# A hybrid decoder layer on one Trainium2 core: later heads' loads ordered behind the last chunk's transfers, a rope table per block, and a re-planned instruction order

## The chip, the core and the metric

The kernel runs on 1 core of one Trainium2 chip. The core has five engines that run side by side: TensorE (PE in the profile, with PEld for its weight loads), VectorE (DVE), ScalarE (ACT), GpSimd (POOL) and SyncE (SP), which in this kernel issues nearly all DMA transfers. Every transfer goes through 16 shared DMA engines. The metric is the time of one execution in microseconds; lower is better.

## The reference

One layer of a decoder on 2048 tokens of width 1024, all in float32:

```python
a   = rmsnorm(x, norm_pre_mix)
proj = a @ w_in                       # 1024 -> 1960 columns
h_ml  = mlstm_chunkwise(silu(conv(qk)), v, gates)        # 4 heads, recurrent over chunks
q = rmsnorm(c_q) @ w_uq ; kv = rmsnorm(c_kv) @ w_ukv     # 8 heads, rope on 32 of 96 columns
h_mla = causal softmax attention(q, k, v)
x = x + rmsnorm(concat(h_ml, h_mla) @ w_out, norm_post_mix)
x = x + rmsnorm(relu(rmsnorm(x) @ w_up)**2 @ w_down, norm_post_mlp)
```

## The kernel before

**Number format.** A float32 product is made of three TensorE passes: each operand is split into a rounded part (`hi`, cast on ACT) and the remainder (`lo`, a subtraction on DVE or POOL), and `mm3` (L225) adds hi·hi, hi·lo and lo·hi. So each loaded weight costs an ACT cast and a DVE or POOL subtraction before TensorE can use it.

**Stages.** (1) Input projections and mLSTM, in four blocks of 512 tokens (`b` = 0 to 3). A block has 16 units of weight columns (`unit`, `values`), small products for q, k and v of the attention heads (`operands`: tiles `kp`, `vp`, `qp`, `rp`), and four recurrent chunks of 128 tokens (`chunk`, L1141). Results for the heads are staged in four `sg` buffers (tiles `ks`, `vs`, `qs`, `rs`) and stored to DRAM (`qkd`, `vd`, `qrd`). (2) Attention over 8 heads × 4 query blocks: row maxima first (`maxima`, tile `m`), then scores `S`, two exponentials on ACT, a low part on DVE or POOL, and the products with `V`. (3) Output projection. (4) The two MLP products.

**The rope table.** `rope_tables` (L1288) computes sines and cosines in two halves `q`, each of which holds two blocks; it stores them to `trigd` (L1334) and spreads them into a table `trep` for all 2048 tokens with six DMAs per half (L1341, 1 MB per half). Each block later reads its part into `tb` (L820).

**The last chunk.** Chunk (3,3) needs the rows `E` (L1157, `load_e`) and `iw` (L1165, `load_w`), broadcast from DRAM. `E` has two buffers, freed by the numerators (L1192, L1193) of two chunks before; `iw` has one, freed by `scale_q` (L1186) of the chunk before. ACT then makes the exponentials (L1172). When the last chunk has ended, `switch3` (L1409) closes its buffers and opens those of the scores `S`.

**Head loads.** `load_qk` (L1495) brings q and k of one head and block into SBUF with three DMAs, `load_v` (L1508) brings V of two key tiles of 128 tokens, for four heads at once, and `matrix` (L1828) loads rows of w_out. All are issued by SP, in one queue, in program order.

**What sets the order.** Nothing runs in the order it is written. Every step is registered with `pl.op(engine, ns, function, after, key, take, free, kb)` (L137): an engine, an assumed duration, what it must follow, a due time (`key`), and the buffers it takes and frees. `Plan.run` (L147) simulates the engines with these durations and issues, for each engine, the operation that can start first, and of several that can, the one with the lowest key. The order that comes out is pinned for PE, ACT, DVE and POOL (`pin`, L236); each engine then works through its list strictly in that order, and so does the DMA queue of SP. The assumed durations thus decide the order but not the real times. Due times of stage 1 come from `kA(b, t)` (L297), which is `KEYA + (b*BLOCK + t)/1.8`.

Of the kernel before, what the change touches and what calls it, by code (L numbers as in the profile page):

```python
# [10 lines left out]
F32 = mybir.dt.float32  # L11
# [7 lines left out]
P = 128  # L19
# [3 lines left out]
TB = 512  # L23
# [10 lines left out]
HB_ = 4  # L34
LB_ = 4
# [17 lines left out]
LEAD = 20.0  # L53
VLEAD = 6.0
# [3 lines left out]
BLOCK = 123.0  # L58
XLEAD = 20.0
WLEAD = 22.0  # L60
SPLIT = 10.0
XS0 = 12.0
XS1 = -60.0
CHUNK = 2.0
# [4 lines left out]
LGAIN = 20.0  # L69
CPOOL = True  # L70
KPOOL = ()
VPOS = (2, 2, 2, 4)
KROT = 50.0
# [10 lines left out]
WSTORE = 10.0  # L84
# [38 lines left out]
class Plan:  # L123


    HOP, DMA, RATE, SUM = 190.0, 1900.0, 359.0, 4900.0
    late = 0.0

    def __init__(self):
        self.ops, self.rings, self.frees = [], {}, {}  # L130
        self.group, self.groups = None, {}
# [5 lines left out]
    def op(self, eng, ns, fn, after=(), key=0.0, take=(), free=(), kb=0):  # L137


        i = len(self.ops)  # L140
        self.ops.append((eng, ns, fn, list(after), key, take, kb))
# [5 lines left out]
    def run(self):  # L147
# [24 lines left out]
        left, moved = len(ops), 0.0  # L172
        while left:
# [31 lines left out]
            end[i] = at[eng] = s + ops[i][1]  # L205
# [12 lines left out]
def trunk(ctx: ExitStack, tc: tile.TileContext, x, xT, pos, wu, wout, wup, wdn, cols, rows, consts, edge, out, dbg=None):  # L218
# [48 lines left out]
    trep = dram.tile([P, 2, SEQ], F32, tag="trep", name="trep")  # L267
# [29 lines left out]
    def kA(b, t):  # L297

        return KEYA + (b * BLOCK + t) / 1.8
# [66 lines left out]
    def xsplit(b):  # L366
        def pair(j):
# [24 lines left out]
            for s in [slice(0, 1), slice(1, 2)] if b == 0 else [slice(0, 2)]:  # L392
                a = pl.op("SP", 500, lambda s=s: load(s), [first], key=kA(b, 0.65 * (2 * j + s.start) - 3 - XLEAD), kb=256 * (s.stop - s.start))
                for k in range(2 * j + s.start, 2 * j + s.stop):
                    at = kA(b, 0.65 * k - 3)
                    c = pl.op("Activation", 690, lambda k=k: hi(k), [a, o_col], at, take=(f"xh{k}",))
                    d = pl.op("DVE", 700, lambda k=k: lo(k), [c], at, take=(f"xl{k}",), free=[] if here else [("awr", first)])
# [44 lines left out]
    def wsplit(b, u):  # L442
# [27 lines left out]
        for s in pieces:  # L470
            n = s.stop - s.start
            a = pl.op("SP", 500, lambda s=s: load(s), [a0_], key=kA(b, at - WLEAD + WHALF * len(first)), kb=n / 2)
            c = pl.op("Activation", n * 0.833 + 110, lambda s=s: hi(s), [a], kA(b, at - SPLIT), take=() if first else ("wh",))
            d = pl.op(
                "Pool" if slow else "DVE", 148 + 2.104 * n if slow else n / 0.96 + 69, lambda s=s: lo(s), [c] + ([d] if first else []), kA(b, at - SPLIT), take=() if first else ("wl",),
# [127 lines left out]
    def latents_in(b):  # L603
# [4 lines left out]
        def one(i):  # L608
# [32 lines left out]
            if b == 0:  # L641
                o = pl.op("Activation", 560, evac, [u["op"], *t.get("o", [])], key, take=take, free=[("mm", u["head"])])
                head = o
                o = pl.op("DVE", 660, norm, [o, o_rsbc[b]], key, free=[("rsbc", o_rsbc[b])])
# [40 lines left out]
        def split(i):  # L685
# [8 lines left out]
            g = pl.op("DVE", 710, lambda: gain(i), [l, o], late, free=[("cbc", l)])  # L694
# [10 lines left out]
    def operands(b, t, o_c, held):  # L705
# [112 lines left out]
        def table():  # L818
            tb["t"] = e2.tile([P, 2, TB], F32, tag="cbc", name=f"tb{b}", bufs=1)
            dma(tb["t"], trep[:, :, bs])  # L820

        o_tb = pl.op("SP", 500, table, [o_rope[2 * (b % 2) + 1], t["gained"]], kA(b, TIME[b][18] - 10), take=("cbc",), kb=512)
# [46 lines left out]
    def rotate(b, t, G):  # L869
# [26 lines left out]
        g = pl.op("SP", 500, load, [o_rope[2 * (b % 2)], G], key, take=("cth",), kb=128)  # L896
# [149 lines left out]
    def conv(b, j):  # L1046
# [39 lines left out]
        for i in range(1, 4):  # L1086
            o = pl.op("DVE", 720, lambda i=i: tap(i), [o], key, free=[("raw", r)])
# [1618 lines left out]
```

## Time and profile before

| | us |
|---|---|
| median of 3 runs (lowest to highest) | 2447.58 (2446.93 to 2453.14) |
| profiled execution, its own time | 2449.75 |
| span of that execution in the trace | 2447.8 |
| PE busy | 2384.2 (97%) |
| DVE busy | 1766.5 (72%) |
| ACT busy | 1360.5 (56%) |
| POOL busy | 835.1 (34%) |

An engine's busy time is the time in which at least one of its instructions ran. A matmul of 128x512 lasts about 0.4 us in the profile, but the next one starts while it drains; the profile's PEclk says what share of full speed TensorE's clock was granted. In the views quoted below, a timeline row gives the start, the duration (of all instructions merged into the row), the engine, the line, the operation and, in brackets, how long the engine stood idle before it and who released it. A windows row gives busy time and instruction count of each engine in a stretch, then the granted clock, the busy share of the DMA engines and their GB/s.

### The profile page before, as it was taken

The page shows a single profiled execution, that of the slowest core. Times are in us where ns is not written, and L with a number is a line of the kernel's source. Part 1 is how long each engine was busy: PE and PEld are TensorE (multiplying, and loading weights), DVE is VectorE, ACT ScalarE, POOL GpSimd, SP SyncE. Part 2 cuts the span into 40 slices and gives each one's busy share as a digit, 9 for nine tenths or more (in the row PEclk, how much of TensorE's full clock was granted, in tenths as well). Part 3 has the DMA queues.
Part 4 walks back from the last instruction along what each step waited for, and adds up shares of the span by engine and source line. Part 5 has one row for each costly group of instructions (what it writes and reads, how often), then busy time and mean ns, then how long its engine had stood idle before and what let it go on. Part 6 is the DMA issues. An engine that isn't in the chain of part 4 may idle for free.

```text
span 2447.8 us, 34049 instructions
## 1 busy us (share of the span) xinstructions
PE 2384.2 (97%) x10915; PEld 1918.2 (78%) x10915; DVE 1766.5 (72%) x3153; ACT 1360.5 (56%) x2645; POOL 835.1 (34%) x713
## 2 busy tenths in 40 slices
PE   8899999999999999999999999999999999999998
PEld 6777787777777777788887888888888888888886
DVE  6766666648888888744866677766666687687889
ACT  5545444436777777644665666756665344343455
POOL 3433434436888788632100000000000232322346
PEclk9999999998999999999999999999999999999999
DMA  6696969797322220466777788756664534535348
GB/s 241 223 314 214 327 231 325 251 257 179 93 58 67 56 53 12 111 211 217 264 209 207 227 281 246 220 171 180 198 195 140 182 126 148 159 125 183 126 132 183
DMA packets 341819, 449.20 MB, mean 184 GB/s; under 512 B 34908, under 2 KB 227432, under 8 KB 341640
## 3 DMA queue, kind: packets, MB, share of 16 engines
q1 hardware_dynamic: 337704, 440.16, 58.2%
q0 software_dynamic: 3936, 6.87, 2.0%
q8 instruction: 86, 1.41, 0.2%
q14 instruction: 93, 0.76, 0.1%
HBM read 295.97 MB, written 153.05 MB: 183 GB/s over the span
## 4 chain that ended last, share of the span: by engine, by line
PE 78%; DVE 7%; DMA 6%; issue 3%; ACT 3%; POOL 2%; SPq 1%; DVEq 0%; ACTq 0%; POOLq 0%
PE mm L226 3%; PE mm L227 3%; PE mm L228 3%; PE S L226 3%; PE o L1622 2%; PE S L227 2%; PE S L228 2%; PE o L1625 2%; PE m L1537 2%; PE mv L227 1%; PE mv L228 1%; PE mv L226 1%; PE op L226 1%; PE op L228 1%; PE op L227 1%
## 5 line engine op out<-in xcount | busy, mean ns | idle before, releaser
L2516 POOL TENSOR_TENSOR y<-vd_0X,y 128x512 f32<-128x512 f32 x7 | 11.3, 1620 | 727.7 <-ACT vd_0X L2513 709.8
L1636 POOL TENSOR_TENSOR t<-t,ph 128x512 f32<-128x512 f32 (+1 forms) x192 | 214.4, 1116 | 17.8 <-ACT ph L1601 7.8
L1601 ACT ACTIVATE ph<-S 128x512 fp32r<-128x512 f32 (+1 forms) x320 | 170.2, 532 | 87.2 <-PE S L228 33.4
L2428 ACT CAST hh<-hr 128x512 fp32r<-128x512 f32 (+1 forms) x208 | 116.2, 567 | 150.5 <-DMA hr<-hd 23.8
L1609 DVE TENSOR_TENSOR pl<-S,ph 128x512 fp32r<-128x512 f32 (+3 forms) x272 | 156.7, 590 | 30.3 <-ACT S L1605 27.7
L226 PE MATMUL mm<-xh,wh 128*128 128x512 f32 x384 | 160.3, 417 | 17.1 <-ACT wh L458 8.4
L227 PE MATMUL mm<-xl,wh 128*128 128x512 f32 x384 | 151.7, 395 | 1.5 <-DVE xl L388 1.5
L228 PE MATMUL mm<-xh,wl 128*128 128x512 f32 x384 | 151.6, 395 | 0.7 <-DVE wl L463 0.7
L2433 DVE TENSOR_TENSOR hl<-hr,hh 128x512 fp32r<-128x512 f32 (+1 forms) x208 | 130.2, 637 | 28.2 <-ACT hh L2428 21.6
L1542 DVE TENSOR_REDUCE mp<-m 128x1 f32<-128x512 f32 x192 | 128.6, 681 | 27.1 <-PE m L1537 27.0
L1605 ACT ACTIVATE S<-S 128x512 f32<-128x512 f32 (+3 forms) x272 | 141.0, 519 | 0.3
L226 PE MATMUL S<-QK 97*128 97x512 f32 (+1 forms) x320 | 122.9, 384 | 6.2 <-DVE pl L1609 4.1
L1622 PE MATMUL o<-ph,V 128*128 128x512 f32 (+1 forms) x320 | 121.0, 378 | 0.2 <-DVE ot L1695 0.2
L1537 PE MATMUL m<-QK 96*128 96x512 f32 (+3 forms) x320 | 113.3, 399 | 6.8 <-ACT vext L1110 2.7
L227 PE MATMUL S<-QK 97*128 97x512 f32 (+1 forms) x320 | 118.3, 370 | 0.0
L228 PE MATMUL S<-QK 97*128 97x512 f32 (+1 forms) x320 | 117.9, 368 | 0.0
L1625 PE MATMUL o<-pl,V 128*65 128x512 f32 (+1 forms) x320 | 114.8, 361 | 0.2
L226 PEld LDWEIGHTS mm<-xh,wh 128*128 128x128 f32 x384 | 73.1, 190 | 38.3 <-ACT wh L458 8.4
L226 PE MATMUL op<-wo,hh 128*128 128x512 f32 x256 | 101.2, 395 | 0.7 <-DVE x L1937 0.7
L2267 ACT ACTIVATE t<-t 128x512 f32<-128x512 f32 x96 | 60.6, 631 | 73.8 <-DVE t L2262 73.2
L228 PE MATMUL op<-wo,hl 128*128 128x512 f32 x256 | 99.9, 390 | 0.0
L227 PE MATMUL op<-wo,hh 128*128 128x512 f32 x256 | 99.8, 390 | 0.0
(6442 smaller groups left out, 7581.2 us busy)
## 6 DMA issues: line engine op xcount, KB each, us to landing
hr<-hd SPq DMA_DIRECT2D x100, 448.0 KB
wr<-in_wu_dram SPq DMA_DIRECT2D x71, 512.0 KB
hd<-t SPq DMA_DIRECT2D x128, 256.0 KB
hd<-ts SPq DMA_DIRECT2D x96, 256.0 KB
wl<-wparts SPq DMA_DIRECT2D x45, 512.0 KB
QK<-qkd SPq DMA_DIRECT2D x32, 512.0 KB
xt<-in_x_dram SPq DMA_DIRECT2D x28, 512.0 KB
xf<-xd SPq DMA_DIRECT2D x40, 256.0 KB
```

The source lines that it names most:

```text
L226: pe.matmul(o, ah, bh, start=start, stop=False)
L227: pe.matmul(o, ah, bl, start=False, stop=False)
L228: pe.matmul(o, al, bh, start=False, stop=stop)
L1537: pe.matmul(ps[:, :n], Qh[s][0:96, q0 : q0 + P], Kh[s][0:96, kb * TB : kb * TB + n], start=True, stop=True)
L1542: vec.tensor_reduce(mp["t"][:, j, kb : kb + 1], ps, axis=AX.X, op=ALU.max)
L1601: act.activation(t["h"][:, :w], t["S"][:, :w], AF.Exp)
L1605: act.activation(t["p"][:, :w], t["S"][:, :w], AF.Exp)
L1609: (pool if by_pool else vec).tensor_tensor(t["l"][:, :w], t["p"][:, :w], f32(t["h"][:, :w]), ALU.subtract)
L1622: pe.matmul(o0, v[:, 0:128], t["h"][:, :w], start=start, stop=stop)
L1625: pe.matmul(o1, v[:, 64:129], t["l"][:, :w], start=start, stop=stop)
L1636: pool.tensor_tensor(to, to, hv, ALU.add)
L2433: vec.tensor_tensor(t["l", m][:, :w], t["r", m][:, :w], f32(t["h", m][:, :w]), ALU.subtract)
```

## The change

Four groups of edits:

1. **Order of loads.** `load_qk` of head 0 for blocks 1 to 3 and `load_v` of key tiles 4 to 7 are placed after the `E` and `iw` loads of chunk (3,3). V of key tiles 8 and up (heads 0 to 3) is placed after the first scores of an earlier query block of head 0, V of heads 4 to 7 after the first scores of head 2, and the first four rows of w_out after the first scores of head 4. These are orders for the planner; the data don't need them.
2. **Rope table.** `trep` becomes four tables of 512 tokens. The six spreading DMAs per half disappear from `rope_tables`; each block spreads its own part with three DMAs (512 KB) shortly before it loads it.
3. **Stage 1 due times.** The hi and lo parts of the weights of block 0 get a due time 20 units of `t` earlier (`SPLIT0`), the gains and low parts of the latents (`LGAIN`) and the rotation of the rope key (`KROT`) a later one, the rotation of block 0 moves from DVE to POOL (`KPOOL`); evacuations of stage 1 get an earlier due time (`EV`).
4. **Planner and buffers.** One more buffer for `ph` and for `pl` in the attention (`HB_`, `LB_`), other lead times, a lower assumed DMA rate, and a rule that a DVE operation marked `DVES` takes longer while POOL runs an operation of 1100 ns or more. Some 30 operations in all stages are marked so.

```diff
-HB_ = 4
-LB_ = 4
+HB_ = 5
+LB_ = 5
-LEAD = 20.0
-VLEAD = 6.0
+LEAD = 25.0
+VLEAD = 3.0
-BLOCK = 123.0
+BLOCK = 119.0
+SPLIT0 = 30.0
-CHUNK = 2.0
+CHUNK = 0.0
-LGAIN = 20.0
+LGAIN = 40.0
-KPOOL = ()
+KPOOL = (0,)
-KROT = 50.0
+KROT = 90.0
-WSTORE = 10.0
+WSTORE = 5.0
-EV = 8.0
+EV = 15.0
-PQ = 0.0
+PQ = 5.0
...
-    HOP, DMA, RATE, SUM = 190.0, 1900.0, 359.0, 4900.0
+    HOP, DMA, RATE, SUM = 190.0, 1900.0, 345.0, 4900.0
+    BESIDE, HEAVY = 0.75, 1100.0
...
+            ns = ops[i][1]
+            if i in self.shared and pool_end > s:
+                both = min(pool_end - s, ns / (1 - self.BESIDE))
+                ns += self.BESIDE * both
+            end[i] = at[eng] = s + ns
+            if eng == "Pool" and ns >= self.HEAVY:
+                pool_end = s + ns
+                if last_shared > s:
+                    at["DVE"] = max(at.get("DVE", 0.0), last_shared) + self.BESIDE * (last_shared - s)
...
-    trep = dram.tile([P, 2, SEQ], F32, tag="trep", name="trep")
+    trep = [dram.tile([P, 2, TB], F32, tag=f"trep{b}", name=f"trep{b}") for b in range(NB)]
...
+            split = SPLIT if b else SPLIT0
-            c = pl.op("Activation", ..., lambda s=s: hi(s), [a], kA(b, at - SPLIT), ...)
+            c = pl.op("Activation", ..., lambda s=s: hi(s), [a], kA(b, at - split), ...)
-                "Pool" if slow else "DVE", ..., kA(b, at - SPLIT), ...
+                "Pool" if slow else "DVES", ..., kA(b, at - split), ...
...
+        def spread():
+            for x, r0, g0, n in ((0, 0, 0, 8), (1, 48, 0, 4), (1, 32, 4, 4)):
+                to = trep[b].rearrange("(g j) x t -> g j x t", j=16)[g0 : g0 + n, :, x]
+                dma(to, trigd[r0 : r0 + 16, bs].rearrange("(o j) t -> o j t", o=1).broadcast_to((n, 16, TB)))
-        o_tb = pl.op("SP", 500, table, [o_rope[2 * (b % 2) + 1], t["gained"]], kA(b, TIME[b][18] - 10), take=("cbc",), kb=512)
+        o = pl.op("SP", 1800, spread, [o_rope[b % 2], t["gained"]], kA(b, TIME[b][18] - 25), kb=512)
+        o_tb = pl.op("SP", 500, table, [o, t["gained"]], kA(b, TIME[b][18] - 10), take=("cbc",), kb=512)
...
-        e = pl.op("SP", 500, load_e, [o_sc_in[b, "wd"]], key, take=("E",), kb=256)
-        i = pl.op("SP", 1000, load_w, [o_sc_in[b, "wd"]], key, take=("iwbc",), kb=128)
+        e = out["e"] = pl.op("SP", 500, load_e, [o_sc_in[b, "wd"]], key, take=("E",), kb=256)
+        i = out["i"] = pl.op("SP", 1000, load_w, [o_sc_in[b, "wd"]], key, take=("iwbc",), kb=128)
...
-        o = pl.op("SP", 1500, load, [..., o_s3 if s else o_s1, *war], key, kb=640)
+        o = pl.op("SP", 1500, load, [..., o_s3 if s else o_s1, *war, *(o_last if b and not h else [])], key, kb=640)
+    o_last = [o_chunk[NB - 1, 3]["e"], o_chunk[NB - 1, 3]["i"]]
...
-        o_v[g, t] = [pl.op("SP", 1000, load, [..., *([o_s3, o_const["v"]] if g else [o_s2, o_const["v0"]])], key, kb=512)]
+        if g:
+            after = [o_s3, o_const["v"], o_sc[start_of[2, qb]]]
+        else:
+            after = [o_s2, o_const["v0"], *([o_sc[start_of[0, qb - 2]]] if qb > 1 else o_last if qb else [])]
+        o_v[g, t] = [pl.op("SP", 1000, load, [o_vd[t], o_vd[t + 1], *after], key, kb=660)]
...
-        a = pl.op("SP", 500, load, [o_s3 if early else o_left], key, take=("wr",), kb=512)
+        a = pl.op("SP", 500, load, [o_sc[start_of[4, 0]] if early else o_left], key, take=("wr",), kb=512)
```

The old `spread` in `rope_tables` (L1336 to L1341, L1355) is taken out.

More of the change, by code (lines that the diff above doesn't have):

```diff
@@ L894, in lo @@
             eng.tensor_tensor(t["Gr"][s], t["G"][s], t["tg"][s], ALU.subtract)
-        g = pl.op("SP", 500, load, [o_rope[2 * (b % 2)], G], key, take=("cth",), kb=128)
+        g = pl.op("SP", 500, load, [o_rope[b % 2], G], key, take=("cth",), kb=128)
         o = pl.op(*cost, d1, [g, G], key)
@@ L1090, in conv @@
         o_qk[b, j] = [
-            pl.op("DVE", 670, lambda i=i: put(i), [h, *war, *(o_fill3 if j < 2 else [])], key, free=[("cy", y), ("cth", h)])
+            pl.op("DVES", 670, lambda i=i: put(i), [h, *war, *(o_fill3 if j < 2 else [])], key, free=[("cy", y), ("cth", h)])
             for i in range(2 if j < 2 else 1)
@@ L2106, in factor @@
         b = pl.op("Activation", 610, hi, [a, opened], key, take=(f"x{i}{kk}h",))
[L2107 removed]
+        c = pl.op("DVES", 690, lo, [b], key, take=(f"x{i}{kk}l",), free=[("xr", a)])
         o_xo[g, i, kk] = [b, c, None]
```

105 lines of the change are left out of this document (52 added, 53 removed).

## The prediction

> **What bounds the kernel.** I read the page's totals first, then busy time by stage, then the list of PE's waits, then the granted clock around the longest waits.
>
> ```profile
> PE 2384.2 (97%) x10915; PEld 1918.2 (78%) x10915; DVE 1766.5 (72%) x3153; ACT 1360.5 (56%) x2645; POOL 835.1 (34%) x713
> ```
> ```profile
> 0.00:138.00 138.00, 116.63 (x511) 92.44 (x512) 95.09 (x184) 72.33 (x133) 54.68 (x54) 0.96 0.71 242
> 138.00:520.00 382.00, 370.08 (x1709) 294.39 (x1708) 239.35 (x492) 178.24 (x346) 154.26 (x139) 1.00 0.80 275
> 520.00:580.00 60.00, 53.96 (x239) 41.70 (x238) 38.60 (x106) 22.21 (x66) 21.40 (x28) 0.83 0.96 231
> 580.00:990.00 410.00, 404.03 (x2072) 307.30 (x2071) 341.60 (x772) 318.49 (x663) 335.46 (x289) 1.00 0.27 63
> 990.00:2370.00 1380.00, 1372.29 (x6101) 1128.55 (x6101) 980.09 (x1501) 723.56 (x1318) 216.59 (x150) 1.00 0.61 187
> ```
> ```profile
> PE mv L227 <- DVE wl L463: 4.9, 2, 3.3
> PE mm L226 <- ACT vs L784: 4.3, 1, 4.3
> PE m L1537 <- ACT vext L1110: 2.7, 1, 2.7
> ```
>
> TensorE is the bound, and the change takes no matmul away. So all it can win is PE's idle time and the time at a reduced clock. Idle is 21.4 us in the first 138 us (the start among them, which stays), 11.9 us up to 520, 6.0 us up to 580, 6.0 us in the attention and 7.7 us up to 2370. These three longest waits after the start fall on places that the change touches. The clock after them:
>
> ```profile
> 64.00:71.00 7.00, 5.42 (x13) 3.69 (x13) 6.86 (x10) 1.80 (x5) 2.79 (x3) 0.52 0.89 268
> 129.00:132.00 3.00, 3.00 (x9) 2.32 (x8) 2.54 (x3) 2.66 (x5) 1.24 (x2) 0.50 0.71 157
> 538.00:542.00 4.00, 1.21 (x7) 0.73 (x5) 1.21 (x2) 3.21 (x13) 2.44 (x5) 0.97 0.96 271
> 542.00:548.50 6.50, 5.91 (x20) 5.14 (x21) 4.53 (x15) 0.00 (x0) 0.83 (x1) 0.50 1.17 294
> 548.50:555.50 7.00, 5.29 (x22) 2.71 (x20) 6.60 (x23) 2.55 (x11) 1.01 (x1) 0.99 0.78 207
> 555.50:569.00 13.50, 13.04 (x39) 9.49 (x40) 8.27 (x20) 4.44 (x11) 3.10 (x7) 0.50 0.94 221
> ```
>
> Each of these waits is followed by a stretch at half clock, which costs about half of the busy time in it: 5.42 × 0.48 = 2.6 us, 1.5 us, 5.91/2 = 3.0 us and 13.04/2 = 6.5 us. So a wait of 3 to 4 us costs more than itself.
>
> **A. Weight splits of block 0.** In the values unit TensorE stands twice for the low parts `wl`:
>
> ```profile
> 53.37 1.05 ACT L458 CAST wh<-wr 128x1024 fp32r<-128x1024 f32 x1 [1.38 <-PE mm L227]
> 55.95 1.41 DVE L681 SCALAR_TENSOR_TENSOR cca<-cca,col,cbc 128x512 f32<-128x512 f32 x2
> 57.27 3.48 DVE L1078 SCALAR_TENSOR_TENSOR qbd<-cth,cy 64x512 f32<-64x512 f32 x2
> 60.78 2.18 DVE L463 TENSOR_TENSOR wl<-wr,wh 128x1024 fp32r<-128x1024 f32 x1
> 65.49 1.22 DVE L463 TENSOR_TENSOR wl<-wr,wh 128x1024 fp32r<-128x1024 f32 x1
> 58.48 3.40 POOL L692 TENSOR_TENSOR cl<-cca,ch 128x512 fp32r<-128x512 f32 x2
> L1078 DVE SCALAR_TENSOR_TENSOR qbd<-cth,cy x16: 671/690/1790, 48.4 to 475.5; 64x512 f32<-64x512 f32 x16
> ```
>
> The cast was done at 54.4, but DVE first made gains (1.41) and two `qbd` writes (3.48). The earlier key puts `wl` ahead of both, so the first wait (3.3) goes. The second weight's cast waits for a buffer that TensorE frees, so I leave the second wait. Of the 2.6 us at half clock I take half: 3.3 + 1.3 = 4.6, say **4.5 us won**. Bounds: nothing (what DVE leaves for later delays chunk 0 as much) to 4.9 + 2.6 = 7.5. No instruction is added here.
>
> Moving the four rotation steps of block 0 to POOL frees DVE of 4 × 0.69 us (the median `qbd` row is the nearest) and gives POOL 4 × 1.3 to 1.7 us (the `cl` row: 3.40 for two). The rows also show a price: beside those `cl` steps a `qbd` write took 1.7 us instead of 0.69. If each moved step stretches one DVE step by 1.1 us, DVE loses 4.4 − 2.8 = 1.6 us. With 43 us of DVE idle in this stage and a later due time, I take 0 for it, between −2.8 and +1.6. [...]
>
> **B. Rope table.** At 112 us the second half's six DMAs stand ahead of the stores that free the `sg` buffers, and at 86 us the first half's stand ahead of an `E` load:
>
> ```profile
> 86.31 4.51 SPq L1341 DMA_DIRECT2D trep<-trigd  x6
> 112.45 4.51 SPq L1341 DMA_DIRECT2D trep<-trigd  x6
> 117.26 1.27 SPq L763 DMA_DIRECT2D qkd<-ks  x2
> 115.96 1.30 POOL L739 TENSOR_TENSOR ks<-ks 128x512 fp32r<-128x512 f32 x1
> ```
> ```profile
> 91.91 7.16 DMA E<-wd
> 117.92 9.13 DMA qkd<-ks
> ```
> ```profile
> 99.09 1.28 ACT L1172 ACTIVATE E<-E,tm 128x128 f32<-128x128 f32 x4 [2.59 <-DMA E<-wd]
> 127.17 0.69 DVE L787 COPY vs<-vp 128x512 f32<-128x512 f32 x1 [2.32 <-DMA qkd<-ks]
> ```
>
> DVE waits for the landing of a store that took 9.13 us, behind 1 MB of table. Without it SP is free at 112.5 and the store has only its own data (done at 117.3) and other transfers to wait for. The `E` landing of 7.16 us, behind another 1 MB, is the nearest row for the same queue with half the table; I put the store's landing 3 us lower. So of the 4.3 us wait 3 goes, 1.5 of clock behind it, and 0.5 at 99 us, where ACT idled 2.59 us: **5.0 us won**, bounds 0 and 4.3 + 1.5 + 0.8 = 6.6.
>
> The cost: blocks 1 to 3 get three DMAs each, 4.51/2 = 2.3 us of SP's queue and 512 KB, in a stretch whose DMA engines are 0.80 busy. The queue delays whatever store or load is next by up to 2.3 us, three times 2.3 = 6.8 at most, and 0 where a load has its usual lead. I take **1.0 us lost**.
>
> **C. The last chunk.** This is the largest term.
>
> ```profile
> 524.73 0.60 PE L1193 MATMUL num<-C,qs 128*128 128x258 f32 x2
> 525.42 1.54 POOL L1186 TENSOR_TENSOR qs<-qbd,iwbc 64x256 f32<-64x256 f32 x2 [1.12 <-PE num L1193]
> 528.37 0.60 SPq L1499 DMA_DIRECT2D QK<-qkd  x1
> 529.01 1.36 SPq L1501 DMA_DIRECT2D QK<-qrd  x2
> 531.09 0.45 SPq L1157 DMA_DIRECT2D E<-wd  x1
> 538.00 1.28 ACT L1172 ACTIVATE E<-E,tm 128x128 f32<-128x128 f32 x4 [9.44 <-DMA E<-wd]
> 540.63 0.68 ACT L1110 ACTIVATE vext<-mv,rsx 128x512 f32<-128x512 f32 x1
> 537.12 0.39 PE L228 MATMUL mv<-wh,xl 128*128 128x512 f32 x1
> 544.90 1.07 PE L1192 MATMUL num<-vext,E 128*128 128x129 f32 x4
> 558.20 0.73 PE L226 MATMUL S<-QK 97*128 97x512 f32 x1
> ```
>
> Chunk 1's numerators free the `E` buffer at 525.3. The load is issued at 531.09, behind head loads, and lands at 538.0, 6.9 us later; ACT, which works in order, stands 9.44 us, with `vext` of the last values queued behind it, and TensorE's 2.7 us wait is for that `vext`. With the new order `E` goes at 525.4 and lands by 525.4 + 6.9 = 532.3 at the latest. Then TensorE's values (until 537.5) set the pace: `vext` by 538.6, the numerators at 538.7 instead of 544.90, so 6.2 us sooner. The chain from there to the first scores (558.20 − 544.90 = 13.3 us) stays, some of it at half clock. Of the 9.5 us that the two half-clock stretches cost I take 0.3, as small, scattered products remain: **9.0 us won**. The bound is all idle from 538 to 569 (2.8 + 0.6 + 1.7 + 0.5) and all 9.5 of clock: 15.0. The other bound is 0.
>
> What is moved behind: a head load is 0.60 + 1.36 = 2.0 us of SP. Three of them now follow `iw`, which can go when POOL's scaling ends at 527.0; so they are issued from about 528.4 to 534.3 and land, at 6.9 us, by 541, when maxima and the last chunk run. Cost 0 to 3, I take **0.5 lost**. V of later heads and w_out leave a stretch with a DMA share of 0.96; their use comes more than 100 us later, under 404 us of TensorE work, at a share of 0.27, so I price them at nothing; uncovered, one load would cost its landing, 7 us.
>
> **D. The rest.** More `ph` and `pl` buffers can win at most the attention's 6.0 us of idle; I take **1.0 won**. The new planner costs reorder DVE, ACT and POOL everywhere. No row prices that: from half the idle of 138 to 520 and of the attention won (−9) to as much lost (+9). I take **1.5 lost**, since each removed delay leaves the next buffer or evacuation to be waited for. After 990 TensorE idles 7.7 us in 1380, so reordering there has little to win.
>
> Sum: −4.5 − 5.0 + 1.0 − 9.0 + 0.5 − 1.0 + 1.5 = −16.5 us. Against the profiled execution's own 2449.75 (span 2447.8 and 1.95 around it) that is 2433.2; the median of the runs lies 2.2 below that execution, so **2431 us**.
>
> **The rivals.**
> 1. *The half clock stays.* The scattered small products throttle TensorE without a long wait. Before the stretch from 555.5 the seven us hold 1.7 us of idle in all, and yet half clock followed: that speaks for it. Then A is worth 3.3, B 3.5, C 6.2, and the sum is −11.0: 2437. [...]
> 2. *All of it goes.* A, B and C near their upper bounds (6.5, 6, 13), with the costs as above: −25.5 + 2 − 3 of the attention, about 2421. The stretches at half clock follow the waits closely, which speaks for it; that chains of small steps remain at 545 to 558 speaks against it.
> 3. *The waits move.* DVE has to do the same steps before chunk 0, so A is 0; half the table still precedes the `E` load, so B is 2; the last chunk's long chain keeps C at 5. With the costs 1.0 + 0.5 + 1.5 and no gain in the attention: −4, 2443.5. DVE 6.86 busy of 7.0 at 64 to 71 speaks for it.
> 4. *The queue blocks the heads: slower.* Head 0's blocks 1 to 3 now stand in SP's queue behind `iw`. If that load goes no sooner than 534 (3 us after the present `E`), they are issued until 540.5 and land at 541 to 547.5; TensorE, done with values at 537.5, has only block 0's maxima and the chunk, stands 5 us and runs the next 13.5 us at half clock as now. With C at +7, A and B moved elsewhere (0) and 3 of costs: about +10, 2457. It decides from `E` issued at 531 or later. Against it: the buffer is free at 525.3, and the planner sees that.
>
> **How the numbers follow.** A difference below 0.3% (7.3 us: 2440.2 to 2454.9) can't be told from no change here. Forecast 0.44; rival 1 0.13, rival 2 0.11, rival 3 0.18, rival 4 0.14. Faster: 0.44 + 0.13 + 0.11 = 0.68. Same: 0.18. Slower: 0.14. The forecast's own range is 2422 to 2440; to hold 8 in 10 it must reach to rivals 1 to 3 with the ±9 of the reordering: 2413 to 2452, with rival 4 left out above and the sum of all upper bounds (2408) below.
>
> **What would show it.** A: the `wl` wait of 3.3 us gone and the clock 1.00 from 64 to 71. B: no wait for `vs` near 124, and three table DMAs per block. C: `E` of the last chunk issued within 1 us of the numerators that free it, ACT's 9.44 us gone, the first scores near 542 on a span that is then some 9.5 us shorter by A and B. It would be wrong if the first scores come at 555 or later, if new PE waits above 2 us appear in blocks 1 to 3, or if the attention's idle time grows.

## The result and the profile after

The changed kernel takes 2427.85 us (median of 6 runs, 2425.71 to 2429.46); the kernel before took 2448.38 beside it (6 runs, 2446.93 to 2453.14). The ratio is 0.9912, 95% interval 0.9900 to 0.9925: 20.5 us faster, 3.2 below the forecast of 2431 and inside its range. The profiled span fell from 2447.8 to 2426.0.

First the totals of the changed kernel's page and its windows by stage. The windows are cut where its stages lie, some 20 us earlier than before towards the end.

```profile
PE 2370.5 (98%) x10915; PEld 1915.0 (79%) x10915; DVE 1749.6 (72%) x3149; ACT 1360.6 (56%) x2645; POOL 833.4 (34%) x717
```
```profile
0.00:138.00 138.00, 123.60 (x555) 97.95 (x555) 106.71 (x191) 80.48 (x145) 64.41 (x62) 1.00 0.75 249
64.00:71.00 7.00, 7.00 (x32) 5.51 (x31) 6.88 (x11) 4.75 (x11) 1.69 (x3) 1.00 0.94 281
520.00:580.00 60.00, 56.08 (x266) 42.94 (x266) 47.33 (x125) 32.92 (x80) 30.84 (x34) 0.89 0.87 200
535.37:549.02 13.65, 13.20 (x40) 9.79 (x40) 8.91 (x23) 4.50 (x11) 3.06 (x7) 0.50 0.90 216
2370.00:2426.00 56.00, 38.81 (x162) 30.84 (x160) 45.16 (x67) 24.15 (x64) 34.23 (x37) 0.88 0.84 158
```

TensorE is busy 123.6 us instead of 116.6 of the first 138, and from 64 to 71 its clock is full where it was 0.52. Before the first scores a stretch of 13.65 us at half clock remains. The clock of the last 56 us is 0.88. Of the two stretches at half clock in it, the one behind the last product costs nothing and stood in the kernel before too; 3.4 us from 2402.46, while TensorE works, are new.

Then, of TensorE's waits, the longest after the start and the longest before the first scores:

```profile
PE d_7X L2505 <- DVE y L2528: 3.0, 1, 3.0
...
PE mt L1595 <- DVE mp L1569: 1.9, 1, 1.9
```

The waits for `wl` in the values unit (4.9 in two), for `vs` (4.3) and for `vext` (2.7) are gone; no single wait for `vs` above 0.7 us is left. One wait of 3.0 us has come, 27 us before the end. The rows of the steps that the prediction named, in the timeline of the changed kernel:

```profile
54.56 1.22 DVE L481 TENSOR_TENSOR wl<-wr,wh 128x1024 fp32r<-128x1024 f32 x1
61.56 1.22 DVE L481 TENSOR_TENSOR wl<-wr,wh 128x1024 fp32r<-128x1024 f32 x1
...
511.01 0.33 SPq L1183 DMA_DIRECT2D E<-wd  x1
515.24 1.27 ACT L1198 ACTIVATE E<-E,tm 128x128 f32<-128x128 f32 x4
526.96 0.61 PE L1218 MATMUL num<-vext,E 128*128 128x129 f32 x4
537.82 0.63 PE L244 MATMUL S<-QK 97*128 97x512 f32 x1
```

The two `wl` begin at 54.56 and 61.56 instead of 60.78 and 65.49. `E` of the last chunk is issued right behind the numerators that free it, and the exponentials start without a wait.

**Where the time went.** The last product into `d_5Z` stands some 40 us before the end. It is the 10801st of TensorE's 10915 matmuls in all fourteen kernels, so it divides the gain in two. Its row before and after, and the last product of all:

```profile
2409.78 0.39 PE L2480 MATMUL d_5Z<-d,hl 128*128 128x512 f32 x1
2438.00 0.39 PE L2480 MATMUL d_7X<-d,hl 128*128 128x512 f32 x1
```
```profile
2380.42 0.39 PE L2507 MATMUL d_5Z<-d,hl 128*128 128x512 f32 x1
2411.70 0.39 PE L2507 MATMUL d_7X<-d,hl 128*128 128x512 f32 x1
```

The changed kernel is 17.9 us ahead at the last chunk's numerators (544.90 to 526.96), 20.4 at the first scores (558.20 to 537.82), 29.4 at this product, and only 21.8 at the end of the span (the two profiled executions lie 1.3 us further apart than the medians, which differ by 20.5). So 29.4 us were won and 7.6 given back in the last 40 us.

The trace divides the time up to this product in three: no matmul running, half of the busy time at half clock (there a 128x512 matmul starts 0.43 us after the one before, 2402.71 and 2403.14 in the changed kernel, and at full clock 0.23 us after it, 1070.49 and 1070.72), and the remainder, which the trace shows as busy at full clock.

| us up to `d_5Z` | before | changed |
|---|---|---|
| TensorE idle | 53.0 | 38.3 |
| lost to half clock | 14.0 | 6.6 |
| remainder | 2342.8 | 2335.5 |

The remainder is 7.3 us shorter with the same number of matmuls (10915). 4.7 of it lies between the last product of the last chunk's numerators and the 300th product of the output projection. A 128x512 matmul at full clock shows as busy for 0.39 us and the next starts 0.23 us after it, so a wait of up to some 0.16 us would show as busy and so hide there; that is argued, not measured.

The experiments are read in the same two columns: the start of this product, and the rest of the span after it.

### The profile page after: what moved, and what is told of

It reads as the page before. It is cut to its first block, busy times and chain, and to the rows that moved or that the text cites. A ratio compares the mean times of both kernels' runs of the same rounds, so it can differ in the third digit from the quotient of the medians.

```text
span 2426.0 us, 33941 instructions
## 1 busy us (share of the span) xinstructions
PE 2370.5 (98%) x10915; PEld 1915.0 (79%) x10915; DVE 1749.6 (72%) x3149; ACT 1360.6 (56%) x2645; POOL 833.4 (34%) x717
## 4 chain that ended last, share of the span: by engine, by line
PE 83%; DVE 5%; DMA 4%; issue 3%; POOL 3%; ACT 2%; SPq 1%; DVEq 0%; POOLq 0%; ACTq 0%
PE mm L244 3%; PE mm L245 3%; PE mm L246 3%; PE o L1649 2%; PE m L1564 2%; PE S L244 2%; PE o L1652 2%; PE S L245 2%; PE S L246 2%; PE op L244 2%; PE op L245 2%; PE op L246 2%; PE mv L244 1%; PE mv L245 1%; PE mv L246 1%
## 5 line engine op out<-in xcount | busy, mean ns | idle before, releaser
L2455 ACT CAST hh<-hr 128x512 fp32r<-128x512 f32 (+1 forms) x208 | 116.2, 567 | 157.4 <-DMA hr<-hd 17.9
```

## The experiments

Each kernel was timed beside the kernel before on the same chip. Here are all twelve at a glance; the two columns on the right come from each one's profiled execution.

| kernel | median us | ratio to before (95%) | `d_5Z` at | rest |
|---|---|---|---|---|
| before | 2448.38 | 1 | 2409.78 | 38.0 |
| changed | 2427.85 | 0.9912 (0.9900 to 0.9925) | 2380.42 | 45.6 |
| *one part taken out of the changed kernel* | | | | |
| a_split10: weight splits late again | 2434.42 | 0.9945 (0.9931 to 0.9958) | 2387.72 | 45.4 |
| a_noshare: planner's rule off | 2443.92 | 0.9978 (0.9967 to 0.9988) | 2403.60 | 38.0 |
| a_trep_once: old spread of the table | 2427.98 | 0.9920 (0.9907 to 0.9934) | 2382.55 | 44.3 |
| a_nolast: head 0 not behind `E`, `iw` | 2430.24 | 0.9928 (0.9916 to 0.9941) | 2383.80 | 44.7 |
| a_loads_early: later V and w_out early | 2431.35 | 0.9929 (0.9914 to 0.9945) | 2385.36 | 44.1 |
| a_nogate: both of these | 2432.12 | 0.9936 (0.9923 to 0.9949) | 2385.39 | 42.2 |
| a_hb4: four `ph`, `pl` buffers | 2434.80 | 0.9945 (0.9928 to 0.9961) | 2390.29 | 42.7 |
| t_nokb: rule without DMA issues | 2420.23 | 0.9890 (0.9876 to 0.9903) | 2379.70 | 37.9 |
| *one part alone in the kernel before* | | | | |
| b_split30: weight splits early | 2459.83 | 1.0050 (1.0036 to 1.0064) | 2420.70 | 37.9 |
| b_rule: the rule | 2447.47 | 0.9996 (0.9988 to 1.0005) | 2399.61 | 46.1 |
| b_last: head 0 behind `E`, `iw` | 2449.56 | 1.0004 (0.9993 to 1.0015) | 2409.23 | 37.8 |
| b_hb5: five buffers | 2442.91 | 0.9976 (0.9967 to 0.9986) | 2400.94 | 37.9 |

The two columns on the right scatter, since each comes from a single execution. The instruction order of b_hb5 is that of the kernel before up to 572 us, on every engine, and yet b_hb5 is 2.8 us ahead at 500 us and 4.7 at the first scores (553.47 for 558.20). The profiled executions also lie off their medians, from 1.4 us above (before) to 2.7 below (a_nogate). So a difference of less than some 5 us in `d_5Z` says little by itself; below, such differences are read from a place up to which the orders agree.

### The weight splits of block 0

```diff
-SPLIT0 = 30.0
+SPLIT0 = 10.0
```

This is a_split10, from the changed kernel; b_split30 gives the kernel before the 30 for block 0 alone.

> The changed kernel with one edit undone: the weight splits of block 0 have their old due time again (SPLIT0 30 to 10). Theory 1, the edit is worth both waits for wl and the half clock behind them, as the shift of the same TensorE instructions says (7.1 us between 59 and 73 us): the waits for wl come back (4.9 us in two), the clock falls to about half from 64 to 71, and the time is 2427.9 + 7 = 2435. Theory 2, the recorded size, 4.5 us, the second wait being due to a buffer: 2432.4, and the shorter wait of 1.6 us is the same with and without the edit. Rival, the steps that DVE has put off come back later in the block: the splits are late again but TensorE at 138 us is within 2 us of the changed kernel, 2428 to 2430.

> The kernel before with the weight splits of block 0 due 20 units of t earlier, that edit alone. Theory 1, it is worth alone what it is worth last (6.5 us, from the run that undoes it): 2442, both waits for wl gone and the clock 1.00 from 64 to 71. Recorded size 4.5: 2444. Rival, without the rule of the planner DVE's other steps (gains beside POOL, raw that frees TensorE's bank) are late in place of wl, as in the changed kernel without the rule, where TensorE waited 5.1 us for raw and 4.2 for kT: 2449 to 2455, slower or no change.

Undone, the edit costs 6.6 us in time and 7.3 by `d_5Z`. The waits of a_split10 and its clock in the values unit:

```profile
PE mv L245 <- DVE wl L481: 4.5, 1, 4.5
```
```profile
64.00:71.00 7.00, 4.09 (x11) 3.06 (x11) 6.93 (x6) 2.00 (x6) 6.84 (x7) 0.76 0.47 140
```

Theory 1 had two waits of 4.9 us together; one of 4.5 comes, and 3.4 us at half clock behind it. The time (2434.4) is theory 1's 2435 and not the recorded size's 2432.4, so the edit is worth more than the first wait. But alone in the kernel before the same edit *costs* 11.5 us. The waits of b_split30 from 50 to 95 us, and its clock behind them:

```profile
PE S L1153 <- DVE kT L1080: 4.9, 1, 4.9
PE mv L226 <- DVE raw L1057: 4.7, 1, 4.7
```
```profile
64.80:71.60 6.80, 6.12 (x14) 4.79 (x15) 6.64 (x11) 1.70 (x3) 0.50 (x1) 0.50 0.79 249
85.30:92.10 6.80, 6.13 (x19) 5.24 (x20) 3.16 (x7) 1.86 (x2) 0.00 (x0) 0.50 0.08 19
```

`wl` is in time, and `raw` (which empties a bank that TensorE needs) and `kT` (which chunk 0 needs) are late in its place: 9.6 us of waits for 4.9, each with 6.8 us at half clock. DVE has the same work and is late with other steps: what the rival of this run expected is what the trace shows.

### The planner's rule

```diff
-    BESIDE, HEAVY = 0.75, 1100.0
+    BESIDE, HEAVY = 0.0, 1100.0
```

This is a_noshare, in which a marked step is planned no longer than before; b_rule puts the rule and its marks into the kernel before.

> The changed kernel with the share by which a marked DVE step is planned longer beside a heavy POOL step set from 0.75 to 0, so the plan is made with the old durations in all stages; everything else stays. Theory 1, the rule brought the 7.5 us of the attention and costs 7.7 at the end (2427.9 less 2420.2 of the kernel whose rule leaves out the DMA issues): attention +7.5, end -7.7, time 2428. Theory 2, the rule costs at the end and brings nothing elsewhere: 2420. Rival, the rule brings time in stage 1 too (weight splits and gains in an order that suits the chip): last numerators more than 3 us later and time above 2430.

> The kernel before with the planner's new rule and its marks alone (a marked DVE step is planned longer beside a heavy POOL step); all due times, buffers, loads and the rope table as before. Taking the rule out of the changed kernel lost 19 us by the third value tile (71 us) and 16.1 in time. Theory 1, the rule is a source of its own: TensorE at 140 us is 8 us or more sooner than in the kernel before, and with 7.7 us lost at the end the time is 2435 to 2445. Theory 2, the rule pays only with the new due times that put gains and rotation elsewhere: TensorE at 140 us within 3 us of before, and with the loss at the end 2450 to 2457. Recorded price of the reordering: 1.5 lost, 2450.

Without the rule the changed kernel loses 16.1 us: 23.2 by `d_5Z`, less the 7.6 that it wins in the rest. It is 19.2 us late already at the third value tile, which the changed kernel begins at 71.14 us. So the rival of this run holds, and both theories fall. Its waits from 50 to 95 us name the same two steps as b_split30: most of the 23.2 us is what the early splits cost without the rule. The DVE and POOL rows:

```profile
PE mv L244 <- DVE raw L1083: 5.1, 1, 5.1
PE S L1179 <- DVE kT L1106: 4.2, 1, 4.2
```
```profile
62.89 0.68 DVE L1083 TENSOR_TENSOR raw<-mm,rsbc 128x512 f32<-128x512 f32 x1
62.54 0.48 POOL L1080 TENSOR_SCALAR raw<-halo 128x3 f32<-128x3 f32 x1 [15.63 <-DMA pi<-in_pos_dram]
63.49 1.40 DVE L700 SCALAR_TENSOR_TENSOR cca<-cca,col,cbc 128x512 f32<-128x512 f32 x2
64.81 5.15 DVE L1095 SCALAR_TENSOR_TENSOR cy<-raw,col,cy 128x512 f32<-128x512 f32 x3
65.99 3.43 POOL L711 TENSOR_TENSOR cl<-cca,ch 128x512 fp32r<-128x512 f32 x2
```

The wait for `raw` is one of order alone: DVE makes `wl`, two `qbd` writes and the first step of the rope table's sines (L1333, at 61.88) ahead of it, and that step frees the buffer whose first columns POOL then writes for `raw` (62.54). POOL had run nothing for 15.63 us, so no POOL step slowed DVE there. Behind `raw` the gains of the latents (L700) come ahead of the taps `cy`, and POOL's `cl` then runs beside these taps: 5.15/3 = 1.72 us each, 2.9 us more than three taps at 0.75. The wait for `kT` has these taps ahead of it, but also the other steps of the sines, which the changed kernel begins only at 73.73. In the changed kernel, with no POOL step beside them, four taps take 2.99, and gains and `cl` come only after them:

```profile
66.81 2.99 DVE L1095 SCALAR_TENSOR_TENSOR cy<-raw,col,cy 128x512 f32<-128x512 f32 x4
71.37 0.74 DVE L700 SCALAR_TENSOR_TENSOR ccb<-ccb,col,cbc 128x512 f32<-128x512 f32 x1
74.69 1.70 POOL L711 TENSOR_TENSOR cl<-ccb,ch 128x512 fp32r<-128x512 f32 x1
```

Alone in the kernel before the rule brings 10.2 us by `d_5Z`, although the wait for `wl` stays:

```profile
PE mv L244 <- DVE wl L480: 5.9, 1, 5.9
```

Then it loses 8.1 in the rest (46.1 for 38.0), and its time is the same as before, 0.9996. Neither theory had 2447.5, and neither has the place. Theory 1 wanted TensorE 8 us ahead at 140 us; product by product against the kernel before, it is 1.6 behind at 74 us, 4.8 ahead at 138, 1.1 behind at 200, 6.3 ahead at the first scores and 10.1 at 1500. The 4.8 come where the rule's plan puts the second half of the rope table (issued at 124.92) behind the first stores of `ks` (108.98): the wait for `vs` is down to 1.4 us there.

The rule and the early splits are both in the changed kernel, and no wait above 1.7 us remains between 50 and 95 us. No run has these two alone, so that the later gains and the rotation play no part in it is not shown.

The rule does spare DVE time: up to `d_5Z` DVE is busy 1714.5 us for the 1734.1 without it, and alone 1714.3 for 1732.3. But up to the 300th product of the output projection it is as busy with the rule as without (778.6 for 778.3, and 775.6 for 776.0). The time is spared behind this product, where TensorE's lead changes by only some 2 us (25.3 to 23.2, and 7.8 to 10.2). By these totals, what the rule won before that is a better order and not spared DVE time.

**The end.** Every kernel with the whole rule needs 42.2 to 46.1 us after `d_5Z`, every kernel without it 37.8 to 38.0. (In the two lowest, a_nogate and a_hb4, TensorE's wait of 3.0 us for `d_7X` stands too, but no half clock follows it.) The last stage adds its result to the output with DMAs that POOL issues (`residual`), planned at 1100 ns, and the rule counts them as heavy POOL steps. One line, in t_nokb, leaves them out:

```diff
-            if eng == "Pool" and ns >= self.HEAVY:
+            if eng == "Pool" and ns >= self.HEAVY and not ops[i][6]:
```

> The changed kernel, but the planner's rule for heavy POOL operations leaves out those that only issue a DMA (the residual stores of the last stage, 1100 ns in the plan). TensorE's order is the same up to its last 230 instructions. Theory 1, the 4.5 to 5 us that the changed kernel gives back at its end (the last matmul is 26.3 us sooner than before, the end of the span only 21.8) come from this rule, which orders two gain steps of finished tiles ahead of the sums that free PSUM, and leaves four multiplications by gpm behind the last matmul: TensorE's wait of 3.0 us for d_7X goes, the clock stays 1.00 near 2402, the end follows the last matmul by about 9.4 instead of 13.9, and the time is 2423. Rival, the end is bound by the stores to out_dram: the last matmul is sooner but the time stays within 1.5 us of 2427.9.

It takes 2420.23 us, 7.6 less than the changed kernel and 28 less than the kernel before, the fastest of all. DVE at the changed kernel's end, in its timeline:

```profile
2399.91 1.41 DVE L2601 SCALAR_TENSOR_TENSOR y<-y,fsm,gpm 128x512 f32<-128x512 f32 x2
2401.23 0.68 DVE L2528 TENSOR_TENSOR y<-d_7X,y 128x512 f32<-128x512 f32 x1
2415.75 1.29 DVE L2582 TENSOR_TENSOR y<-y,gpm 128x512 f32<-128x512 f32 x2
2418.28 1.29 DVE L2582 TENSOR_TENSOR y<-y,gpm 128x512 f32<-128x512 f32 x2
```

And t_nokb's end, with the same steps and its last product:

```profile
2397.87 0.68 DVE L2528 TENSOR_TENSOR y<-d_7X,y 128x512 f32<-128x512 f32 x1
2404.77 0.68 DVE L2582 TENSOR_TENSOR y<-y,gpm 128x512 f32<-128x512 f32 x1
2407.49 0.68 DVE L2582 TENSOR_TENSOR y<-y,gpm 128x512 f32<-128x512 f32 x1
2407.82 0.39 PE L2507 MATMUL d_7X<-d,hl 128*128 128x512 f32 x1
```

In the changed kernel DVE scales finished tiles (L2601) ahead of the sum (L2528) that frees TensorE's bank (the wait of 3.0 us shown above, then 3.4 us at half clock), and all four multiplications by `gpm` come behind the last product. In t_nokb two of them come ahead of it and the wait is gone. From `d_5Z` to the last product it needs 28.1 us for 31.3, from there to the end 9.8 for 14.3: 7.7 us in the traces, all of the gain. Theory 1 is shown, and it had 4.9.

### Order of the loads around the last chunk

```diff
-        o = pl.op("SP", 1500, load, [..., *war, *(o_last if b and not h else [])], key, kb=640)
+        o = pl.op("SP", 1500, load, [..., *war], key, kb=640)
-            after = [o_s2, o_const["v0"], *([o_sc[start_of[0, qb - 2]]] if qb > 1 else o_last if qb else [])]
+            after = [o_s2, o_const["v0"], *([o_sc[start_of[0, qb - 2]]] if qb > 1 else [])]
```
```diff
-            after = [o_s3, o_const["v"], o_sc[start_of[2, qb]]]
+            after = [o_s3, o_const["v"]]
-            after = [o_s2, o_const["v0"], *([o_sc[start_of[0, qb - 2]]] if qb > 1 else o_last if qb else [])]
+            after = [o_s2, o_const["v0"], *(o_last if qb else [])]
-        a = pl.op("SP", 500, load, [o_sc[start_of[4, 0]] if early else o_left], key, take=("wr",), kb=512)
+        a = pl.op("SP", 500, load, [o_s3 if early else o_left], key, take=("wr",), kb=512)
```

The first is a_nolast, the second a_loads_early; a_nogate has both. b_last puts the two waits on `o_last` into the kernel before, without the second group. In a_loads_early and in b_last V of key tiles 8 and up (heads 0 to 3) also stands behind `E` and `iw`, other than the expectations below say.

> The changed kernel without the order of head loads behind the last chunk's E and iw (QK of head 0 for blocks 1 to 3 and V of key tiles 4 to 7 may go earlier again). Theory 1: SP issues these loads first, E of the last chunk is issued about 5 us after its buffer is free, ACT stands 6 us or more for it, the first scores come 6.3 us later, and the time is 2434. Recorded size 9.0 less 0.5: 2436.4. Rival, the other due times (CHUNK 0, LEAD 25) put E ahead already: E is issued within 1 us of its buffer, first scores within 1 us, time 2428.

> The changed kernel in which V of key tiles 8 and up, V of heads 4 to 7 and the first rows of w_out may be loaded as early as before; head 0's QK and V of key tiles 4 to 7 stay behind the last chunk's E and iw. Theory 1, these loads compete with the last chunk and the first heads for the queue and the DMA engines: V's issues stand in SP's queue before 560, the first scores or the first blocks of the attention come 2 to 4 us later, 2430 to 2432. Theory 2, the recorded price of nothing: first scores and the attention within 1 us, 2428.

> The changed kernel with the whole order of loads undone: head 0's QK and V of key tiles 4 to 7, V of later tiles and heads and the first rows of w_out may all be loaded as early as before. One part undone cost 2.3, the other 3.4. Theory 1, the parts add: 2433.7. Recorded, 9.0 less 0.5: 2436.4. Rival, they are one thing, DMA and queue freed for the last chunk, and either part undone loses most of it: 2431 to 2432.

> The kernel before with one edit alone: QK of head 0 for blocks 1 to 3 and V of key tiles 4 to 7 are ordered behind E and iw of the last chunk. Theory 1, as the shift of TensorE's instructions says (6.3 us between the last values and the first scores): E is issued within 1 us of the numerators that free it instead of 5.8 us after them, ACT's 9.44 us wait goes, the first scores come 6 us sooner and the time is 2442, with a half-clock stretch of some 13 us still there. Recorded size: 9.0 less 0.5, 2440. Rival, from the run without this edit (only 4.1 us at the first scores): the due times of the chunk bring the rest, so here 4 us, 2444.5.

In a_nolast the load of `E` goes 4.1 us later and ACT waits for it again:

```profile
515.07 1.55 SPq L1183 DMA_DIRECT2D E<-wd  x1
521.72 1.28 ACT L1198 ACTIVATE E<-E,tm 128x128 f32<-128x128 f32 x4 [6.58 <-DMA E<-wd]
```

The 6.65 us from issue to use are near the prediction's landing of 6.9. a_loads_early loses too, although `E` goes as early as in the changed kernel (at 513.05 on an axis that is 2.0 us later): now V and w_out stand in SP's queue around the first scores, and head 1's loads behind them.

In time a_nolast loses 2.4 us, a_loads_early 3.5 and a_nogate 4.3, and the intervals of all three overlap that of the changed kernel. So the traces have to decide. PE, ACT, DVE and POOL have one order in all four kernels up to 530 us, and yet the numerators of the chunk before the last begin at 518.29, 520.54 and 517.35 for the changed kernel's 518.50. Counted from there, the first scores (541.74, 544.23 and 545.03 for 537.82) come 4.1, 4.4 and 8.4 us later, and `d_5Z` 3.6, 2.9 and 6.1.

So at the first scores the parts add, as theory 1 of a_nogate had it, and by `d_5Z` they nearly do; its rival, one thing, had 2431 to 2432, and the time of 2432.12 (2429.16 to 2437.60) does not exclude either. a_loads_early and a_nogate get some 3.5 us back between 750 and 1020 us; why is not shown. Theory 1 of a_nolast was right in kind (`E` 4.1 us later, ACT standing 6.58) and too large (6.3 at the first scores, 2434). In a_loads_early the recorded price of nothing fails at the first scores.

Much of it is clock. a_nogate before its first scores:

```profile
527.70:531.10 3.40, 3.40 (x14) 2.93 (x13) 1.64 (x7) 0.00 (x0) 0.00 (x0) 0.50 1.01 263
534.50:555.00 20.50, 18.89 (x55) 13.02 (x56) 16.16 (x40) 4.73 (x12) 4.12 (x8) 0.50 0.95 238
```

Half of the busy time is (3.40 + 18.89)/2 = 11.1 us; in the changed kernel it is 13.20/2 = 6.6.

In the kernel before, the edit alone brings nothing (1.0004). `E` goes at once (525.40), the first scores are 5.2 us sooner (553.0 for 558.2), and the gain is lost 30 us later at a new wait and its clock, in b_last's waits from 545 to 605, its timeline and its windows:

```profile
PE o L1624 <- DVE ot L1697: 3.0, 1, 3.0
```
```profile
578.24 1.06 SPq L1707 DMA_DIRECT2D hT<-ot  x1
584.15 0.58 ACT L1694 COPY ot<-o 64x512 f32<-64x512 f32 x1 [3.50 <-DMA hT<-ot]
```
```profile
586.40:589.80 3.40, 3.30 (x11) 2.27 (x10) 2.22 (x6) 2.42 (x6) 3.15 (x4) 0.50 1.07 276
```

The order of PE, ACT, DVE and POOL is that of the kernel before throughout. ACT stands 3.50 us for the landing of a store of `ot`, which frees the buffer, and this store goes only 1.8 us sooner than before (578.24 for 580.00), behind eight DMAs of V in SP's queue. So the queue holds the heads up once more, with V of heads 4 to 7, which the second group moves behind the first scores of head 2. All three figures expected of b_last (2440 to 2444.5) were wrong.

### Buffers of the attention

```diff
-HB_ = 5
-LB_ = 5
+HB_ = 4
+LB_ = 4
```

This is a_hb4, from the changed kernel; b_hb5 is the reverse edit in the kernel before.

> The changed kernel with four buffers again for ph and pl in the attention instead of five. Between the first scores and the first product of the output projection the changed kernel is 7.5 us shorter than the kernel before, where the prediction had 1.0 for the buffers. Theory 1, the buffers are the cause: this stretch is 5 to 7 us longer than the changed kernel's, time 2433 to 2435, with TensorE waiting for pl or mp. Theory 2, the recorded 1.0: stretch 1 us longer, 2429. Theory 3, the order of DVE and POOL by the new rule of the planner is the cause: no difference here, 2428.

> The kernel before with five buffers for ph and pl in the attention instead of four, alone. Theory 1, from the run with four in the changed kernel (6.9 us longer): 2442, TensorE's wait of 2.8 us for pl at the end of the attention (985 to 1045) gone. Recorded size 1.0: 2448. Rival, in the kernel before the attention is not limited by these buffers, and what four buffers cost in the changed kernel are waits of 1.7 us each with a half-clock window behind (3.4 us at 799 and 1000), which the order there happens to meet: 2447 to 2450.

One more buffer of each is worth 6.9 us in time in the changed kernel and 5.3 in the kernel before. By `d_5Z` it is 9.9 and 8.8, of which 1.2 and 4.7 stood already at the first scores, up to which the orders agree: 8.6 and 4.1 are left. Of the four parts tried alone it is the only one that shortens the time, and theory 1 has the time right in both. Its stretch in a_hb4 it has not: from the first scores to the first product of the output projection nothing changes (432.9 for 433.0), the loss shows up to the 300th of these products. And in b_hb5 the wait of 2.8 us for `pl` goes, but one of 2.3 for POOL's `pl` comes. a_hb4's waits from 780 to 1050, and the clock around the two longest:

```profile
PE o L1652 <- POOL pl L1636: 2.0, 2, 1.7
PE S L244 <- DVE pl L1636: 1.7, 1, 1.7
```
```profile
795.80:799.20 3.40, 1.84 (x10) 1.53 (x11) 3.17 (x10) 1.63 (x6) 2.38 (x3) 0.99 0.30 110
799.20:802.61 3.41, 3.41 (x14) 2.49 (x13) 2.27 (x8) 3.04 (x7) 2.23 (x3) 0.51 0.19 39
997.10:1000.50 3.40, 1.65 (x7) 1.03 (x7) 1.60 (x4) 2.03 (x4) 3.38 (x3) 1.00 0.86 293
1000.50:1003.91 3.41, 3.41 (x10) 2.71 (x9) 1.86 (x4) 2.13 (x4) 3.17 (x4) 0.51 0.15 52
```

Each of these waits of 1.7 us costs itself and 1.7 of clock. Between the last product of the last chunk's numerators and the 300th product of the output projection a_hb4 needs 547.5 us for 536.2: 4.2 more idle, 4.7 more at half clock and 2.4 more of the remainder. In b_hb5 this stretch is 6.2 shorter than before (537.9 for 544.1): 0.9 idle, 0.4 clock, and 4.9 of time that the trace shows as busy.

### The rope table

```diff
-        o = pl.op("SP", 1800, spread, [o_rope[b % 2], t["gained"]], kA(b, TIME[b][18] - 25), kb=512)
-        o_tb = pl.op("SP", 500, table, [o, t["gained"]], kA(b, TIME[b][18] - 10), take=("cbc",), kb=512)
+        o_tb = pl.op("SP", 500, table, [o_spread[b % 2], t["gained"]], kA(b, TIME[b][18] - 10), take=("cbc",), kb=512)
...
             o_rope.append(o)
+            o_spread.append(pl.op("SP", 3000, spread, [o], key, kb=1024))
```

In this kernel, a_trep_once, six DMAs spread each half behind its sines again; the four tables stay.

> The changed kernel with the rope table spread as before: six DMAs per half of the table behind the sines, the four tables kept. Theory 1, the shift of the same TensorE instructions: DVE waits again for the landing of the ks store near 120 us, TensorE for vs, and the time is 3.6 us longer, 2431.5. Recorded size: 5.0 won less 1.0 for the per-block DMAs, so 4.0 longer here, 2431.9; the shift in blocks 1 to 3 would then become 0.3 us smaller per block. Rival, the planner moves the stores ahead of the table anyway because other due times have changed: no wait above 2 us near 120, time within 1.5 us of the changed kernel.

The time is the same (2427.98 for 2427.85); the 2.1 us lost by `d_5Z` are within the scatter. The stores now stand ahead of the table in SP's queue, so the wait for `vs` does not come back:

```profile
112.09 3.51 SPq L782 DMA_DIRECT2D qkd<-ks  x4
117.64 4.38 SPq L1360 DMA_DIRECT2D trep<-trigd  x6
```

That is the rival: the rest of the plan has moved the stores, and the new spread adds little to it. In b_rule, with the old table, the planner's rule alone does so.

## Why the prediction was right, and where its steps failed

The forecast of 2431 was right in sign and within 3.2 us, and its signs A to C came, but most of its terms had the wrong size and their errors cancelled. That the sum came so near is luck.

**A, weight splits, −4.5.** The signs to look for came: the wait of 3.3 gone, the clock 1.00 from 64 to 71. The term was too small (7.3 by `d_5Z`): "the second weight's cast waits for a buffer that TensorE frees, so I leave the second wait" failed, since the second `wl` came 3.9 us sooner too, and all of the half clock went, not half. And its lower bound, "nothing (what DVE leaves for later delays chunk 0 as much)", was wrong in kind: alone the edit loses 11 us, because it puts `raw` and `kT` late. Rival 3 described that mechanism and priced A at zero for it.

**The rotation on POOL, 0.** It was not tried by itself. The price beside it, 1.7 us for a `qbd` write next to POOL's `cl` and 0.69 for the median one, was the most telling row of the profile, and the prediction used it for this small edit alone. The new rule puts this price into the plan.

**B, rope table, −5.0 + 1.0.** The `vs` wait of 4.3 us went, but the spread is not what removes it in the changed kernel: with the old spread it stays away, and the time is the same. The step that failed is the premise that the stores would stay behind the table unless the table was moved.

**C, the last chunk, −9.0 + 0.5.** `E` was issued at once and ACT's 9.44 us went. The numerators came 17.9 us sooner where the changed kernel was already 13.9 ahead on the chunk before, so 4.0 for the 6.2 taken; the half clock there fell from 9.5 us to 6.6, so 2.9, which is what was taken (0.3 of 9.5). a_nolast, which undoes this part alone, puts the first scores back by 4.1.

"V of later heads and w_out … I price them at nothing" failed: moving these loads is worth 4.4 us at the first scores and, net of the start, 2.9 by `d_5Z`. Taken whole, the order of loads is worth 8.4 at the first scores, 6.1 by `d_5Z` and 4.3 in time, for 8.5.

**D, buffers, −1.0.** "Can win at most the attention's 6.0 us of idle" failed. The idle time of a stage is no bound: in a_hb4 two waits bring half clock of their own, and in b_hb5 4.9 of the 6.2 us won there had been shown as busy; what TensorE lost in those stays open. Measured: 6.9 us in time, 5.3 alone.

**D, reordering, +1.5 (±9).** This is the largest error. The rule is worth 23.2 us by `d_5Z` in the changed kernel, 19.2 of them at the values of block 0, and 10.2 alone, and it costs some 8 in the last 40 us. "After 990 … reordering there has little to win" was true and left out that it can lose.

**The rivals.** Rival 1 is half right: the half clock stays at the first scores (13.65 us) and goes at the two other places. Rival 4 is excluded, `E` being issued 20 us before its limit of 531, or 6 on an axis that is 13.9 us shorter. A mark of the prediction that proved right is that no wait above 2 us came in blocks 1 to 3.

**The parts don't add.** Splits and rule act on the same waits. Taken out one at a time, splits, rule, table, loads and buffers lose 7.3 + 23.2 + 2.1 + 5.0 + 9.9 = 47.5 us by `d_5Z`, and together they brought 29.4. Put in alone, splits, rule, head 0's order and buffers bring −10.9 + 10.2 + 0.6 + 8.8 = 8.7. Each figure scatters by some us. The other due times, leads and the assumed DMA rate were not tried by themselves.

## What to carry to other kernels

Where a plan orders the work, price an edit of a due time together with what the engine then does later, and bound it on the losing side as well: here the wait taken from `wl`, with DVE 6.86 of 7.0 us busy in the kernel before, came back at `raw` and `kT`, 9.6 us for 4.9. When the plan is taught what the profile shows (here a tap beside POOL's `cl` took 1.72 us, not 0.75), look where time is won: here the spared DVE time lay where TensorE did not wait, and the gain came from the new order. Check which operations the new rule catches: here DMA issues counted as POOL work and cost 7.7 us. Find a product near the end whose place in the order is the same in all kernels and read gains on both sides of it; a span alone would have hidden that 29 us were won and 8 lost. Then see how far two executions of the same order differ (here up to 4.7 us) before reading small differences.

## What the runs showed of the hardware

The half clock came in steps of one length. Up to the last product its stretches last 3.41, 6.83, 13.65, 17.07 or 20.5 us, and in the kernel before they start at 63.93, 128.79, 541.80 and 555.45, which is 19, 121 and 4 steps of 3.413 apart. If the trace is cut into windows of this length, so that each stretch begins with one, half clock also followed windows in which TensorE worked: in a_hb4 windows with 1.84 and 1.65 us of busy time in 3.40 were each followed by one at half clock. One of 1.67 in 3.50 in the changed kernel (453.40 to 456.90) was not.

The fourteen traces together, cut into these windows from 15 us to the last product, show the edge. All 28 windows at full clock with TensorE busy for less than 0.47 of them were followed by half clock, 8 of the 29 between 0.47 and 0.54, and 13 of the 9700 above that, one in each of thirteen kernels, just ahead of the first scores (busy 0.60 to 0.83). Of these, the kernel before and the changed one have 4 of 4 below 0.47 (0.07 to 0.27), none of 4 from 0.49 to 0.53, and 2 of 1388 above (2.63 us of 3.41 from 552.04, 2.06 from 531.96). So about half a window was the edge here, and a wait near it may or may not cost as much again: two of 1.7 us did in a_hb4, and one of 1.79 in the changed kernel (for `ks`, up to 457.48) did not. Around the first scores half clock lasts four to six windows although TensorE is shown busy for 0.70 to 1.00 of each (2.96 us of 3.41 in the first of the changed kernel, all of the other three); why is not shown.
